# The second block's first norm: weighted x is transposed before its root is known, and the root's factor is applied behind the projections

## The chip, the cores and the metric

The kernel runs as one program on one core of a Trainium2 chip. The metric is the device time of one execution in microseconds (us); of several executions the median is taken. The engines are called as the profile calls them: PE is TensorE's matrix multiply, PEld its weight load, DVE is VectorE, ACT is ScalarE, POOL is GpSimd, SP is SyncE (here it issues the weight loads). Times inside the trace are us from the start of the span.

## The reference

A sequence of 256 tokens of width 1024, everything in float32. The first block has two layers (attention, layer norm, a mixture of 16384 experts called PEER, layer norm). The second block follows on its output:

```python
def rms_norm(x, gain):
    y = xf * lax.rsqrt(jnp.mean(xf * xf, axis=-1, keepdims=True) + NORM_EPS)
    return y * gain

# first_block, last step of its second layer
x = _layer_norm(DEEPNORM_ALPHA * x + ffn, ln_g[layer, 1], ln_b[layer, 1])

# second_block
u = rms_norm(h, attn_pre_norm[l])
mix = hybrid_mixer(u, w_in[l], ...)      # proj = u @ w_in, split into q, k, v, x_lru, g_lru, 2 gates
h = h + rms_norm(mix, attn_post_norm[l])
u = rms_norm(h, mlp_pre_norm[l])
h = h + rms_norm(jnp.square(jax.nn.relu(u @ w_mlp_up[l])) @ w_mlp_down[l], mlp_post_norm[l])
```

The place of the change is the seam between the two blocks: a layer norm, the weighted root mean square norm of its result, and the first projection of `u @ w_in`.

## The kernel before

Tokens lie in two blocks `b` of 128 on the partitions. Each weight of 128x1024 is loaded in float32 (`raw`, four buffers, SP's queue), split into a rounded part `hi` on ACT (L66) and the rest `lo` on DVE (L67), and multiplied in three passes: `hi` with `xh`, `lo` with `xh`, `hi` with `xl`. `xh` and `xl` are the same two parts of the activations, transposed, so that the 1024 features lie on the partitions. The weights come in one fixed list (`plan`); `Stream.next` hands out the next one and splits ahead of it up to two more. The parts have three buffers (`PARTS`), so the `hi` of weight n+3 can only be written when PE is through with weight n. All engines work in the order in which the code is written (a manual schedule); background generators (`bg`) get one step at each `tick`.

A junction between two stages goes like this (`layer_norm`): the last DEFER weights of the projection before are held back for the second block, so that block 0's accumulators end early (`finish`). While PE works on the held matmuls (L182), DVE does block 0's norm. Then come block 0's two halves `h` of 512 columns: four transposes each (L300) into PSUM, a cast to `xh` on ACT (L163) and a subtraction to `xl` on DVE (L164). `half_pass(0)` multiplies block 0 with the first four weights of the next stage (24 matmuls of 512 columns, L157 to L159), while DVE does block 1's norm; `half_pass(1)` does the same for block 1, and in it the next three weights are split.

At three of the junctions of this form the layer norm's own result is transposed. At the one in front of the second block, `begin` returns a function that calls `pre_norm` for each block first: mean square (ACT squares with a sum, L927), root (`rsqrt`: ACT logarithm and exponential, L266 and L267, and one Newton step on DVE, L270 to L273), the product with the gain (L940, L942), the product with the root `pnr` (L944 on DVE for the first half, L945 on ACT for the second), and only then the transposes. `jd` takes the first 512 columns of q (L257); five `proj_half` calls of four weights each do the rest of q, k and v (20 weights, 12 matmuls of 512 columns each, evacuated by ACT at L229 as two tiles); `rope` rotates q and k on DVE (12 small operations, L1033 to L1035) after its half is evacuated. The other four projections (x_lru, the two gates, g_lru) are transposed ones (`proj_t`) and read the same `xh`, `xl`.

`block2` begins with small loads on POOL's queue (cos, sin, the columns `cv`, the mask; L1010 to L1018). The first of them waits for the last matmul of `half_pass(1)`, whose buffers it takes over. Near the end of the mixer POOL's queue loads x (`spill`) and two gains (L1216, L288) for the next norm.

## Time and profile before

| | us |
|---|---|
| median of three runs | 2264.73 (2263.79 to 2266.92) |
| the profiled execution's own time | 2268.64 |
| its span in the trace | 2266.5 |
| PE busy | 2218.0 (98%) |
| DVE busy | 1757.2 (78%) |
| ACT busy | 1229.8 (54%) |

PE is busy nearly all the time, so a stage's time is its matmuls' time unless a wait of PE shows. The three runs spread over 3.1 us. The profiled execution is 3.9 us above their median and its span 1.8 us above; 2.1 us of its time lie outside the span.

### The profile page before, as it was taken

To read this page: it belongs to the slowest core of one execution; us is meant where nothing else is said; L and a number is where in the kernel's file an instruction comes from. 1 tells how busy PE (TensorE), PEld (TensorE's weight loads), DVE (VectorE), ACT (ScalarE), POOL (GpSimd) and SP (SyncE) were. 2 spreads that over 40 slices of the span, in tenths; PEclk is the share of its full clock that TensorE was granted. 3 is DMA by queue.
4 is the path that set the end of the run, shared out by engine and by line. 5 is a ranking of instruction groups with operands and counts; after the bars stand their busy time and mean duration, and the time that the engine had idled before them with its cause. 6 is when DMAs were issued, how large, how long until landed. Compare 5 with 4: busy or idle time off the path is not lost.

```text
span 2266.5 us, 39922 instructions
## 1 busy us (share of the span) xinstructions
PE 2218.0 (98%) x15028; PEld 2000.1 (88%) x15028; DVE 1757.2 (78%) x3501; ACT 1229.8 (54%) x2115; POOL 54.8 (2%) x118
## 2 busy tenths in 40 slices
PE   8999999999999999999999999999999999999998
PEld 7779999999888887888999999888888779997986
DVE  6879998887766668677999988776666857886754
ACT  5744455666445544674445566644555546765643
POOL 4200000000000000000000000000000000000000
PEclk9999999999999999999999999999999999999999
DMA  7556676556777777545667655777777655565664
GB/s 252 156 173 233 218 234 223 201 196 237 253 242 240 243 239 249 185 139 177 226 231 233 216 204 191 255 242 243 243 241 248 218 186 161 178 184 176 214 187 138
DMA packets 151666, 481.96 MB, mean 213 GB/s; under 512 B 17856, under 2 KB 18400, under 8 KB 150192
## 3 DMA queue, kind: packets, MB, share of 16 engines
q1 hardware_dynamic: 126288, 423.09, 57.9%
q10 hardware_dynamic: 19008, 34.61, 4.1%
q0 software_dynamic: 6176, 21.70, 2.7%
q8 instruction: 118, 1.93, 0.3%
q14 instruction: 76, 0.62, 0.1%
HBM read 437.39 MB, written 39.85 MB: 211 GB/s over the span
## 4 chain that ended last, share of the span: by engine, by line
PE 85%; DVE 5%; issue 4%; ACT 3%; DMA 3%; POOL 0%; ACTq 0%; DVEq 0%; SPq 0%; POOLq 0%
PE ps_acc L182 31%; PE ps_h L157 15%; PE ps_h L159 15%; PE ps_h L158 15%; DVE lo L67 1%; PE ps_acc L821 1%; PE ps_acc L822 1%; PE ps_acc L157 1%; PE ps_acc L158 1%; PE ps_acc L159 1%; ACT hi L66 1%; DMA raw<-peer_v 1%; PE ps_acc L705 0%; DMA raw<-peer_w_q 0%; DVE lns L319 0%
## 5 line engine op out<-in xcount | busy, mean ns | idle before, releaser
L67 DVE TENSOR_TENSOR lo<-raw,hi 128x1024 fp32r<-128x1024 f32 x740 | 901.5, 1221 | 415.7 <-ACT hi L66 412.2
L66 ACT CAST hi<-raw 128x1024 fp32r<-128x1024 f32 x740 | 774.6, 1050 | 432.7 <-issue 290.7
L157 PE MATMUL ps_h<-xh,hi 128*128 128x256 f32 x2784 | 788.6, 283 | 1.0 <-ACT k L628 1.0
L159 PE MATMUL ps_h<-xh,lo 128*128 128x256 f32 x2784 | 773.2, 278 | 3.4 <-DVE lo L67 3.3
L158 PE MATMUL ps_h<-xl,hi 128*128 128x256 f32 x2784 | 773.2, 278 | 0.0
L157 PEld LDWEIGHTS ps_h<-xh,hi 128*128 128x128 f32 x2784 | 525.7, 189 | 6.1 <-issue 1.7
L159 PEld LDWEIGHTS ps_h<-xh,lo 128*128 128x128 f32 x2784 | 522.9, 188 | 4.2 <-DVE lo L67 4.2
L158 PEld LDWEIGHTS ps_h<-xl,hi 128*128 128x128 f32 x2784 | 523.3, 188 | 0.2
L182 PE MATMUL ps_acc<-hi,wh 128*128 128x512 f32 x1024 | 318.2, 390 | 3.4 <-ACT wh L163 3.3
L182 PE MATMUL ps_acc<-hi,wo 128*128 128x512 f32 x1024 | 318.0, 390 | 0.1
L182 PE MATMUL ps_acc<-lo,wh 128*128 128x512 f32 x1024 | 317.4, 389 | 0.2 <-DVE lo L67 0.2
L848 ACT ACTIVATE hs<-ps_h 128x256 f32<-128x256 f32 x256 | 98.3, 384 | 343.6 <-PE ps_h L159 176.8
L182 PEld LDWEIGHTS ps_acc<-hi,wh 128*128 128x128 f32 x1024 | 191.5, 188 | 45.6 <-ACT wh L163 6.2
L182 PEld LDWEIGHTS ps_acc<-hi,wo 128*128 128x128 f32 x1024 | 191.7, 188 | 41.4 <-DVE wo L164 1.9
L182 PEld LDWEIGHTS ps_acc<-lo,wh 128*128 128x128 f32 x1024 | 192.1, 188 | 40.6 <-DVE lo L67 0.7
L164 DVE TENSOR_TENSOR wo<-jd,wh 128x256 fp32r<-128x256 f32 x256 | 107.1, 419 | 2.0 <-ACT wh L163 2.0
L872 DVE TENSOR_TENSOR jd<-G,jd 128x256 f32<-128x256 f32 x256 | 106.9, 417 | 2.2 <-ACT G L824 2.2
L163 ACT CAST wh<-jd 128x256 fp32r<-128x256 f32 x256 | 101.7, 397 | 11.0 <-DVE jd L872 10.9
L824 ACT ACTIVATE G<-ps_acc 128x64 f32<-128x64 f32 (+1 forms) x256 | 82.1, 385 | 6.6 <-PE ps_acc L822 1.0
L157 PE MATMUL ps_h<-hi,xh 128*128 128x512 f32 x160 | 68.8, 430 | 9.5 <-ACT hi L66 7.8
L821 PE MATMUL ps_acc<-oh 128*128 128x128 f16 x512 | 69.6, 221 | 0.0
L822 PE MATMUL ps_acc<-oh 128*128 128x128 f16 x512 | 68.6, 219 | 0.0
(358 smaller groups left out, 2372.6 us busy)
## 6 DMA issues: line engine op xcount, KB each, us to landing
raw<-peer_u SPq DMA_DIRECT2D x256, 512.0 KB, 4.5
raw<-peer_v SPq DMA_DIRECT2D x256, 512.0 KB, 4.3
H<-hs SPq DMA_DIRECT2D x128, 256.0 KB, 2.1
jd<-H ACTq DMA_DIRECT2D x128, 256.0 KB, 4.2
raw<-w_in SPq DMA_DIRECT2D x32, 512.0 KB, 3.7
raw<-w_up SPq DMA_DIRECT2D x32, 512.0 KB, 4.0
raw<-w_down SPq DMA_DIRECT2D x32, 512.0 KB, 4.2
raw<-w_qkv SPq DMA_DIRECT2D x24, 512.0 KB, 4.4
```

What stands on the lines that cost most here:

```text
L66: self.nc.scalar.copy(hi, raw)
L67: self.nc.vector.tensor_sub(lo, raw, hi)
L157: mm(out, lh, rh, start=start, stop=False)
L158: mm(out, lh, rl, start=False, stop=False)
L159: mm(out, ll, rh, start=False, stop=stop)
L163: self.nc.scalar.copy(hi, src)
L164: self.nc.vector.tensor_sub(lo, src, hi)
L182: mm(acc[half], x, w[:, half * 512 : half * 512 + 512], start=a, stop=b)
L821: mm(out, o[:, 0, j], o[:, 1, j], start=True, stop=False)
L822: mm(out, o[:, 0, j], o[:, 2, j], start=False, stop=True)
L848: nc.scalar.activation(hs[i // 2][:, i % 2], o, AF.Gelu)
L872: nc.vector.tensor_tensor(w, g[:, i - first], hl[i // 2][:, i % 2], ALU.mult)
```

## The change

`pre_norm` is gone. `norm` takes a function `then` that it calls after each half: it multiplies the layer norm's result with the gain into the buffer `y`, and `y` is transposed without its root. `layer_norm` computes the root's factor aside with `late_factor` (the sums of squares on ACT behind the casts of the same block, the rest of both blocks behind block 1's transposes) into a lasting tile `factor`, and `half_pass` and `proj_half` multiply with it, token by token, when ACT evacuates q, k and v. The transposed projections have the tokens on the free dimension, where a factor for each partition doesn't help; for them `rescale`, a background generator, adds `xh` and `xl`, multiplies with the factor spread over all partitions (`rb`), and splits the product again into `x2`. The factor comes into `rb` by way of DRAM: two small transfers on POOL's queue behind the mask. `x2` lies where x and the two gains are loaded later, so that load now waits for the last matmul that reads `x2`.

```diff
@@ proj_half, half_pass
-            self.nc.scalar.copy(dst[:, b], acc[b])
+            if by is None:
+                self.nc.scalar.copy(dst[:, b], acc[b])
+            else:
+                self.nc.scalar.mul(dst[:, b], acc[b], by[:, b : b + 1])
@@ norm
             nc.vector.scalar_tensor_tensor(x[:, b, s], y[:, s], r, beta[:, s], ALU.mult, ALU.add)
+            if then:
+                then(y, s)
@@ layer_norm
+            def scaled(b):
+                def then(y, s):
+                    u[b] = y
+                    nc.vector.tensor_tensor(y[:, s], x[:, b, s], gain[:, s], ALU.mult)
+
+                return then
+
+            factors = [self.late_factor(pool, x[:, b], self.factor[:, b : b + 1]) for b in range(NB)]
-        u0 = after(0) if after else x[:, 0]
-        n1 = self.norm(pool, 1, acc[1], x, g, beta)
+        n1 = self.norm(pool, 1, acc[1], x, g, beta, scaled(1))
         for h in range(2):
             next(n1)
-            self.transposed(0, h, u0)
+            self.transposed(0, h, u[0])
         self.st.split(self.st.used + NJ, self.st.used)
+        if factors:
+            next(factors[0])
         next(n1)
         self.half_pass(0, tiles)
-        u1 = after(1) if after else x[:, 1]
         for h in range(2):
-            self.transposed(1, h, u1)
-        self.half_pass(1, tiles)
+            self.transposed(1, h, u[1])
+        if factors:
+            next(factors[1])
+            for f in factors:
+                for _ in f:
+                    pass
+        self.half_pass(1, tiles, self.factor if factors else None)
@@ pre_norm (removed)
-        root = self.mean_square(pool, r, [x[:, s] for s in halves], 1e-6)
-        next(root)
-        nc.vector.tensor_tensor(u[:, halves[0]], x[:, halves[0]], gain[:, halves[0]], ALU.mult)
-        next(root)
-        nc.vector.tensor_tensor(u[:, halves[1]], x[:, halves[1]], gain[:, halves[1]], ALU.mult)
-        next(root)
-        nc.vector.tensor_scalar(u[:, halves[0]], u[:, halves[0]], r, None, ALU.mult)
-        nc.scalar.mul(u[:, halves[1]], u[:, halves[1]], r)
@@ block2
+            rx = outer.enter_context(tc.tile_pool(name="b2x", bufs=1, side="right"))
+            x2 = [rx.tile([P, KD, T], F32R, tag=t, name="x2" + t) for t in ("x", "gains")]
+            rd = self.dram.tile([NB, P], F32, tag="rd", name="rd")
+            rb = two.tile([P, 2, T], F32, tag="th", name="rb")[:, 0]
+            nc.gpsimd.dma_start(rd.rearrange("b p -> p b"), self.factor)
+            nc.gpsimd.dma_start(rb, rd.rearrange("b p -> (b p)").unsqueeze(0).to_broadcast([P, T]))
+
+            def rescale():
+                for _ in range(4):
+                    yield
+                for k in range(0, KD, 2):
+                    s = slice(k, k + 2)
+                    z = two.tile([P, 2, T], F32, tag="m2", name=f"xz{k}")
+                    nc.vector.tensor_tensor(z, self.xh[:, s].bitcast(F32), self.xl[:, s].bitcast(F32), ALU.add)
+                    yield
+                    nc.vector.tensor_tensor(z, z, rb.unsqueeze(1).to_broadcast([P, 2, T]), ALU.mult)
+                    self.part(x2[0][:, s], x2[1][:, s], z)
+                    yield
...
-                        self.proj_half(self.xh, self.xl, dst[:, :, half * 512 : half * 512 + 512], "acc")
+                        self.proj_half(self.xh, self.xl, dst[:, :, half * 512 : half * 512 + 512], "acc", self.factor)
...
-                    o = self.proj_t(self.xh, self.xl)
+                    o = self.proj_t(*x2)
...
-            xp = outer.enter_context(tc.tile_pool(name="b2x", bufs=1, side="right"))
-            x = xp.tile([P, NB, D], F32, tag="x", name="x2")
+            x = rx.tile([P, NB, D], F32, tag="x", name="x2")
             nc.gpsimd.dma_start(x, spill)
```

Three places show how the order of instructions moves. The first is DVE at block 0's norm, from the layer norm's first half on (`lny` is the norm's buffer y, `xr` its result, `pnu` the weighted and scaled copy, `mss` the sum of squares, `pnr` the root, `ps_acc` the accumulators, `xl` the small part of the transposed activations). Before:

```order
L329 SCALAR_TENSOR_TENSOR xr_19675<-lny_21194,lnr_21197,gains_20812 128x512
L323 SCALAR_TENSOR_TENSOR lny_21194<-lny_21194,lnm_21196,gains_20812 128x512
L329 SCALAR_TENSOR_TENSOR xr_19675<-lny_21194,lnr_21197,gains_20812 128x512
L940 TENSOR_TENSOR pnu_21217<-xr_19675,gains_20813 128x512
L929 TENSOR_TENSOR mss_21219<-mss_21219 128x1
L268 TENSOR_SCALAR rsx_21224<-mss_21219 128x1
L942 TENSOR_TENSOR pnu_21217<-xr_19675,gains_20813 128x512
L270 SCALAR_TENSOR_TENSOR rsz_21226<-rsy_21225,rsx_21224 128x1
L271 TENSOR_SCALAR rsz_21226<-rsz_21226 128x1
L273 TENSOR_TENSOR pnr_21216<-rsy_21225,rsz_21226 128x1
L944 TENSOR_SCALAR pnu_21217<-pnu_21217,pnr_21216 128x512
L316 SCALAR_TENSOR_TENSOR lny_21236<-xr_19675,ps_acc_18169 128x512
```

Now, at the same place:

```order
L336 SCALAR_TENSOR_TENSOR xr_19676<-lny_21195,lnr_21198,gains_20813 128x512
L351 TENSOR_TENSOR lny_21195<-xr_19676,gains_20814 128x512
L330 SCALAR_TENSOR_TENSOR lny_21195<-lny_21195,lnm_21197,gains_20813 128x512
L336 SCALAR_TENSOR_TENSOR xr_19676<-lny_21195,lnr_21198,gains_20813 128x512
L351 TENSOR_TENSOR lny_21195<-xr_19676,gains_20814 128x512
L323 SCALAR_TENSOR_TENSOR lny_21219<-xr_19676,ps_acc_18170 128x512
L165 TENSOR_TENSOR xl<-ps_m_21224,xh 128x4x128
```

The first half's product with the gain stands right behind the first half of the norm, and nothing of the root stands ahead of block 1's first step (L316 before, L323 now).

The second place is ACT behind block 1's transposes, from the casts to `xh` to the evacuation of `half_pass` (`hi` are weights of the first `proj_half`, `msj` the squares, `fac` the factor). Before:

```order
L163 CAST xh<-ps_m_21323 128x4x128
L163 CAST xh<-ps_m_21330 128x4x128
L66 CAST hi_21344<-raw_21279 128x1024
L66 CAST hi_21354<-raw_21287 128x1024
L66 CAST hi_21364<-raw_21295 128x1024
L257 COPY jd<-ps_h_21272 128x512
L257 COPY jd<-ps_h_21337 128x512
```

Now:

```order
L164 CAST xh<-ps_m_21292 128x4x128
L164 CAST xh<-ps_m_21299 128x4x128
L954 ACTIVATE msj_21306,mss_21307<-xr_19676 128x512 x2
L273 ACTIVATE rsy_21312<-mss_21240,eps1e-06_76 128x1
L274 ACTIVATE rsy_21312<-rsy_21312 128x1
L273 ACTIVATE rsy_21322<-mss_21307,eps1e-06_76 128x1
L274 ACTIVATE rsy_21322<-rsy_21322 128x1
L66 CAST hi_21337<-raw_21268 128x1024
L66 CAST hi_21347<-raw_21276 128x1024
L66 CAST hi_21357<-raw_21284 128x1024
L264 ACTIVATE jd<-ps_h_21261,fac 128x512
L264 ACTIVATE jd<-ps_h_21330,fac 128x512
```

Block 1's squares and both blocks' roots stand ahead of the three weight splits, and the evacuation is a product instead of a copy.

The third place is DVE in the projections of k, from the weights split in the second `proj_half` to its `rope` (`xz` is `rescale`'s buffer z, `x2x` and `x2gains` the two parts of `x2`, `kn` is k). Only rows of the change are new here; before, the four rows `lo` and the `rope` stood alone.

```order
L1048 TENSOR_TENSOR xz_21557<-xh,xl 128x512
L67 TENSOR_TENSOR lo_21562<-raw_21539,hi_21561 128x1024
L1050 TENSOR_TENSOR xz_21557<-xz_21557,rb 128x512
L165 TENSOR_TENSOR x2gains<-xz_21557,x2x 128x512
L67 TENSOR_TENSOR lo_21583<-raw_21559,hi_21582 128x1024
L1048 TENSOR_TENSOR xz_21598<-xh,xl 128x512
L67 TENSOR_TENSOR lo_21603<-raw_21580,hi_21602 128x1024
L1050 TENSOR_TENSOR xz_21598<-xz_21598,rb 128x512
L165 TENSOR_TENSOR x2gains<-xz_21598,x2x 128x512
L1067 TENSOR_TENSOR rm_21623<-kn_21388,cos_21402 128x64
```

Between the weights' small parts there are now an addition, a product that waits for `rb`, and a subtraction that waits for a cast on ACT; the second and the fourth of these sets stand right ahead of a `rope`.

## Rows read from the trace of the kernel before

**Rows 1.** The page: its first line, the busy time of each engine, and the shares of the span in the chain of work that ended last.

```profile
span 2266.5 us, 39922 instructions
PE 2218.0 (98%) x15028; PEld 2000.1 (88%) x15028; DVE 1757.2 (78%) x3501; ACT 1229.8 (54%) x2115; POOL 54.8 (2%) x118
...
PE 85%; DVE 5%; issue 4%; ACT 3%; DMA 3%; POOL 0%; ACTq 0%; DVEq 0%; SPq 0%; POOLq 0%
```

**Rows 2.** The waits of PE between 1780 and 2000 us: who waited for whom, us in total, times, the longest.

```profile
PE ps_m L300 <- DVE pnu L944: 5.1, 2, 3.0
PE ps_h L159 <- DVE lo L67: 3.3, 2, 2.8
```

**Rows 3.** PE's instructions at the seam in order of time: start, duration, engine, line, operation, in brackets the idle time before and what ended it. The held matmuls' last, block 0's transposes, the first matmul of `half_pass(0)`, block 1's transposes, the first matmul of `half_pass(1)`, and the first two of the first `proj_half`.

```profile
1799.33 0.39 PE L182 MATMUL ps_acc<-hi,wo 128*128 128x512 f32 x1
1802.69 1.97 PE L300 MATMUL ps_m<-ident,pnu 128*128 128x128 f32 x8 [2.97 <-DVE pnu L944]
1804.48 0.79 PE L157 MATMUL ps_h<-hi,xh 128*128 128x512 f32 x1
...
1814.35 1.07 PE L300 MATMUL ps_m<-ident,pnu 128*128 128x128 f32 x8 [2.12 <-DVE pnu L944]
1815.66 0.80 PE L157 MATMUL ps_h<-hi,xh 128*128 128x512 f32 x1 [0.24 <-ACT xh L163]
...
1822.82 0.39 PE L157 MATMUL ps_acc<-hi,xh 128*128 128x512 f32 x1
1823.05 0.40 PE L158 MATMUL ps_acc<-lo,xh 128*128 128x512 f32 x1
```

**Rows 4.** Two stretches of 2 us, one in each half pass: the stretch, its length, busy time (and instructions) of PE, PEld, DVE, ACT and POOL, then the granted clock of PE as a share of full speed, the DMA share and GB/s.

```profile
1804.00:1806.00 2.00, 2.00 (x8) 1.45 (x7) 1.54 (x3) 1.01 (x2) 0.00 (x0) 0.50 0.00 0
...
1816.00:1818.00 2.00, 2.00 (x6) 1.48 (x6) 1.86 (x3) 2.00 (x4) 0.00 (x0) 0.50 0.00 0
```

**Rows 5.** DVE's instructions at the seam in order of time, with the columns of rows 3.

```profile
1797.60 0.75 DVE L329 SCALAR_TENSOR_TENSOR xr<-lny,lnr,gains 128x512 f32<-128x512 f32 x1
1798.27 0.74 DVE L323 SCALAR_TENSOR_TENSOR lny<-lny,lnm,gains 128x512 f32<-128x512 f32 x1
1799.05 0.75 DVE L329 SCALAR_TENSOR_TENSOR xr<-lny,lnr,gains 128x512 f32<-128x512 f32 x1
1799.72 0.68 DVE L940 TENSOR_TENSOR pnu<-xr,gains 128x512 f32<-128x512 f32 x1
...
1805.66 0.68 DVE L164 TENSOR_TENSOR xl<-ps_m,xh 128x512 fp32r<-128x512 f32 x1
1806.26 1.27 DVE L319 BATCH_NORM_STATS2 lns<-lny 128x6 f32<-128x512 f32 x2
...
1809.17 0.75 DVE L329 SCALAR_TENSOR_TENSOR xr<-lny,lnr,gains 128x512 f32<-128x512 f32 x1
...
1817.07 3.50 DVE L67 TENSOR_TENSOR lo<-raw,hi 128x1024 fp32r<-128x1024 f32 x3
```

**Rows 6.** PE's instructions at two junctions of the same form without the weighted norm: the first layer's (from 129 us) and the second layer's (from 1029 us). Columns as in rows 3.

```profile
129.06 0.66 PE L300 MATMUL ps_m<-ident,x 128*128 128x128 f32 x4 [1.36 <-DVE x L329]
...
131.23 0.40 PE L158 MATMUL ps_h<-lo,xh 128*128 128x512 f32 x1
...
1029.27 0.63 PE L300 MATMUL ps_m<-ident,x 128*128 128x128 f32 x4 [0.87 <-DVE x L329]
1029.66 0.48 PE L157 MATMUL ps_h<-hi,xh 128*128 128x512 f32 x1
...
1035.62 0.60 PE L300 MATMUL ps_m<-ident,x 128*128 128x128 f32 x4
```

**Rows 7.** ACT's instructions at the seam: squares with a sum, the root's logarithm, the product with the root, the three weight splits, and a copy out of PSUM. Columns as in rows 3.

```profile
1809.96 0.63 ACT L927 ACTIVATE msj<-xr 128x512 f32<-128x512 f32 x1 [1.61 <-DVE xr L329]
...
1812.42 0.29 ACT L266 ACTIVATE rsy<-mss,eps1e-06_76 128x1 f32<-128x1 f32 x1 [0.23 <-DVE mss L929]
...
1813.72 0.72 ACT L945 ACTIVATE pnu<-pnu,pnr 128x512 f32<-128x512 f32 x1 [0.77 <-DVE pnr L273]
...
1815.98 2.95 ACT L66 CAST hi<-raw 128x1024 fp32r<-128x1024 f32 x3
...
1823.02 0.59 ACT L257 COPY jd<-ps_h 128x512 f32<-128x512 f32 x1 [3.60 <-PE ps_h L159]
```

**Rows 8.** The second `proj_half` ends (tiles of k): ACT's evacuation of two tiles, then DVE's row `lo` before the `rope`, the first of the `rope`'s twelve operations, and the next `lo`. Columns as in rows 3.

```profile
1844.31 1.27 ACT L229 COPY kn<-ps_acc 128x512 f32<-128x512 f32 x2 [1.01 <-PE ps_acc L159]
...
1843.33 1.23 DVE L67 TENSOR_TENSOR lo<-raw,hi 128x1024 fp32r<-128x1024 f32 x1 [1.52 <-ACT hi L66]
1844.93 0.22 DVE L1033 TENSOR_TENSOR rm<-kn,cos 128x64 f32<-128x64 f32 x1 [0.37 <-ACT kn L229]
...
1846.87 1.22 DVE L67 TENSOR_TENSOR lo<-raw,hi 128x1024 fp32r<-128x1024 f32 x1
```

**Rows 9.** POOL's queue: the first of the small loads and the mask behind them, and the later load of x. Columns as in rows 3.

```profile
1823.53 0.54 POOL L1010 DMA_DIRECT2D cos<-c_cos  x1 [11.32 <-DMA raw<-w_qkv]
...
1827.81 0.59 POOL L1018 DMA_DIRECT2D mask<-c_mask  x1
...
1946.78 0.53 POOL L1216 DMA_DIRECT2D x<-xs  x1 [0.36 <-issue]
```

**Rows 10.** DMA issues of the whole run: what is written from what, the queue, how many, KB each, median us from issue to landing.

```profile
tri_in<-c_tri POOLq DMA_DIRECT2D x1, 128.0 KB, 5.7
...
gcol<-subln SPq DMA_DIRECT2D x1, 0.5 KB, 3.6
```

More of the change, by code (lines that the diff above doesn't have):

```diff
@@ L238, in junction, with half_pass @@
         return ctx
-    def half_pass(self, b, tiles):
+    def half_pass(self, b, tiles, by=None):
         acc = self.ps("h")
@@ L256, in half_pass @@
             for i, ps in enumerate(self.passed):
-                self.nc.scalar.copy(self.jd[:, i, :512], ps)
+                if by is None:
+                    self.nc.scalar.copy(self.jd[:, i, :512], ps)
+                else:
+                    self.nc.scalar.mul(self.jd[:, i, :512], ps, by[:, i : i + 1])
             self.passed = []
@@ L304, in transposed, with norm @@
         self.part(xh[sl], xl[sl], v)
-    def norm(self, pool, b, acc, x, g, beta):
+    def norm(self, pool, b, acc, x, g, beta, then=None):
         nc = self.nc
@@ L329, in norm, with layer_norm @@
             nc.vector.scalar_tensor_tensor(x[:, b, s], y[:, s], r, beta[:, s], ALU.mult, ALU.add)
+            if then:
+                then(y, s)
         yield
[L332 to L339 removed]
+    def layer_norm(self, pool, acc, x, g, beta, gain=None):
+        nc, tiles, factors = self.nc, [], []
+        if gain is not None:
+            u = [None] * NB
+            def scaled(b):
[4 more added lines that the diff above has]
+            factors = [self.late_factor(pool, x[:, b], self.factor[:, b : b + 1]) for b in range(NB)]
+        else:
+            u, scaled = [x[:, b] for b in range(NB)], lambda b: None
+        for _ in self.norm(pool, 0, acc[0], x, g, beta, scaled(0)):
+            pass
+        n1 = self.norm(pool, 1, acc[1], x, g, beta, scaled(1))
         for h in range(2):
             next(n1)
[L342 removed]
+            self.transposed(0, h, u[0])
         self.st.split(self.st.used + NJ, self.st.used)
+        if factors:
+            next(factors[0])
         next(n1)
         self.half_pass(0, tiles)
[L346 removed]
         for h in range(2):
[L348 to L349 removed]
+            self.transposed(1, h, u[1])
[5 more added lines that the diff above has]
+        self.half_pass(1, tiles, self.factor if factors else None)
     def plan(self):
```

28 lines of the change are left out of this document (12 added, 16 removed).

## The prediction

> **What bounds the kernel now.** I began with the page: PE is busy for 98% of the span and has 85% of the chain that ended last [rows 1]. So a change pays what it takes out of PE's waits, or out of matmuls that run at a low clock, and nothing else. Next came PE's waits around the seam: the largest are two on the weighted, scaled copy `pnu`, 5.1 us together; a wait for a weight's small part, 2.8 us at most, lies elsewhere [rows 2]. In order of time PE ends the held matmuls at 1799.72, stands for 2.97 us, transposes block 0, multiplies, stands for 2.12 us, transposes block 1, and starts `half_pass(1)` at 1815.66 and the first `proj_half` at 1822.82 [rows 3]. [...] DVE is what PE waits for: from 1797.60 on it works through norm, product, root and scaling almost without a gap [rows 5].
>
> **The change, part by part.** All starting times are put beside those of before.
>
> *Block 0.* From DVE's rows I take three spacings: 0.78 us to an operation that needs the one right ahead of it (1798.27 to 1799.05), 0.67 us behind a norm step that isn't needed next (1797.60 to 1798.27), 0.60 us behind a two-tensor operation (1805.66 to 1806.26) [rows 5]. The new order gives: norm half 1797.60, product with the gain 1798.38 (ready 1799.06), centre 1798.98, norm half 1799.76, product 1800.54 (ready 1801.22). The first half's transposes follow the held matmuls without a wait, the second's start at about 1801.4, and `half_pass(0)` 0.39 us later (1029.27 to 1029.66 [rows 6]), at 1801.8 instead of 1804.48. Block 1's first step on DVE comes at 1801.14; with it, its second half and two subtractions (four operations, 0.60 us apart) the statistics start at 1803.54 instead of 1806.26: 2.7 us won.
>
> *Block 1.* From the statistics to the first norm half it was 1809.17 - 1806.26 = 2.91 us [rows 5], so that half comes at 1806.45, its product at 1807.23, and after 0.60, 0.78 and 0.78 us the second product at 1809.39, ready at 1810.07. [...] The last four transposes start at about 1810.2, `half_pass(1)` at 1810.6 instead of 1815.66: **5.06 us won**. Here the root, 1.3 us from its logarithm to the scaling (1812.42 to 1813.72 [rows 7]), the scaling itself and the squares have left the path.
>
> *The clock.* PE now stands for about 1.2 us ahead of block 0's second half and 1.55 us ahead of block 1's. Before, 2.97 and 2.12 us were followed by half clock; elsewhere a wait of 1.36 us and the one after it were followed by matmuls of 0.40 us, full clock, and one of 0.87 us too [rows 3, 4, 6]. 1.55 us is nearer to 1.36 than to 2.12, so I take full clock: `half_pass(1)` lasts 5.96 us and ends at 1816.6 instead of 1822.82, 6.2 us won by then.
>
> *What the root costs where it went.* On ACT the squares of block 1 (two of about 0.7 us with the reading of their sums), then two roots, stand ahead of the three weight splits that the first `proj_half` needs. The last cast to `xh` ends at 1811.45, the squares at 1812.9, the first root at 1814.15, the second's exponential at 1814.85. The first `hi` is done 1.05 us later, at 1815.9, its `lo` 1.22 us after that, at 1817.15. PE's second matmul of that weight needs it: 1817.2 instead of 1823.05. So 0.4 us of the clock's gain goes back, and **5.85 us** stay. The next two `lo` come 1.14 us apart [rows 5], against 2.75 us in which PE uses up a weight (12 matmuls, 0.23 us apart, 1822.82 to 1823.05 [rows 3]); they are not late.
>
> *Evacuations.* Ten copies of 128x512 out of PSUM and two of `half_pass` become products. A copy takes 0.59 us, a product with a factor 0.72 us from SBUF [rows 7]; no row has one from PSUM, so 0 to 0.13 us more each. I take the middle; PE has four accumulators there for two in use, so it is hidden, but it delays the `rope` behind it. [...]
>
> *Rescale.* Four times: an addition (0.60 us of DVE), and a set of product, cast on ACT and subtraction, 0.68 + 0.58 + 0.60 and hand-overs, 1.95 us in DVE's order. DVE has 2.75 - 1.14 = 1.6 us per weight to spare and two weights of lead, so a single set is hidden. The tight place is sets two to four, which come with two `rope`s (1.94 us: 1844.93 to 1846.87 [rows 8]). In before's times: the cast of set two waits for both evacuations (from 1844.31 [rows 8]), so the next `lo`, at 1846.87 before, starts at 1848.7. From there to the `lo` of the fifteenth weight DVE has four `lo` (4.6 us), two additions (1.2), a set with a wait for the `hi` behind its cast (2.35), a full set (1.95) and a `rope` (1.94): 12.0 us, so it ends at 1848.7 + 12.0 + 1.2 = 1861.9. PE wants it at 1822.82 + 14 x 2.747 + 0.23 = 1861.5. I charge **0.5 us**; bounds 0 (hand-overs shorter, evacuations as fast as the copy) and 2.
>
> *The factor's way to `rb`.* The mask was issued at 1827.81, 4.3 us behind the queue's first load, which waits for the end of `half_pass(1)` [rows 9]. That end moves by 6.2 us, so the two new transfers follow at 1822.1. Nearest rows: 0.5 KB in pieces of 4 bytes takes 3.6 us, 128 KB into all partitions 5.7 us [rows 10]. With 3.6 to 5.7 us each and 0.5 us of issue, `rb` is there between 1829.8 and 1834. DVE's first product that reads it comes at about 1833.2, and the `lo` behind it has 2.5 us to spare: free.
>
> *x and the gains* were loaded at 1946.78 [rows 9]; now they wait for the last projection of g_lru, some 55 us later, and are needed 65 us after that. I take nothing.
>
> *Sum.* 5.06 + 1.2 (clock) - 0.4 (first `lo`) - 0.5 (fifteenth `lo`) = 5.4 us. The stages behind keep their spacing, so the end moves by as much: the span from 2266.5 to 2261.1. The profiled execution was 3.9 us above the median of the runs, so I put the difference against the median: 2264.73 - 5.4 = **2259.3**.
>
> **The rivals.** A measurement of this kernel can tell about 0.2%, 4.5 us, from no change.
>
> 1. *As above*: 2259.3, with the bounds of the small terms 2258.3 to 2260.4. Chance 0.60.
> 2. *The clock falls all the same.* If `half_pass(1)` still takes 7.16 us it ends at 1817.8, later than the first `lo`, and only the 5.06 us count: 2264.73 - 5.06 + 0.5 = 2260.2. For it: two waits lie close together, and 1.55 us is longer than any in rows 6. Against it: those rows. 0.15.
> 3. *DVE runs full in the projections.* Were each of the four sets late by 0.5 to 1 us on PE's clock instead of one, the loss is 2 to 4 us: about 2262. For it: DVE has no gap there in my count from 1846 to 1861. Against: two weights of lead. 0.11.
> 4. *Given back later.* The later load of x and gains (2 MB) meets the weights of the next stage, or a stage that DVE bounds has slack that swallows the start: about 2264.7. Before, the same 2 MB met the projections and no wait of PE for a weight came of it there [rows 2]. 0.10.
> 5. *Slower: `rb` is late.* Its product stands in DVE's order ahead of every `lo`, so PE stops for as long as it is late beyond 1835.7. The gain of 5.9 us is gone at 1841.6; it is slower by 0.2% from 1846.1, which needs 24 us for the two transfers, against 7.7 to 12. Price there: 2269.3. 0.04.
>
> **How the numbers follow.** The predicted time is the first case's. Both first cases lie near the bound of 2260.2: of the first I count 0.85 as faster by over 0.2%, of the second half: 0.51 + 0.08 = 0.59; with a little for a better fall of the small terms 0.60. Slower by over 0.2%: 0.04. The rest, 0.36, is within it. The range takes in cases 1 to 3 and the spread of medians, about 1 us: 2257.6 to 2263.0, and leaves out cases 4 and 5. The likeliest case's own range is 2258.3 to 2260.4.
>
> **What would show it.** Right: block 0's first transposes with no wait, waits of PE of 1.2 and 1.55 us instead of 2.97 and 2.12 (in place of the waits on L944, waits on the product with the gain), granted clock 1.00 in both half passes, `half_pass(1)` 5 us earlier, a wait of PE for `lo` of about half a microsecond at the first and at the fifteenth weight. Wrong: clock 0.50 again; waits of PE for `lo` at most weights of k; DVE waiting for `rb`; the seam 6 us shorter and a later stage longer by as much.

## The result, and the profile after

The changed kernel takes 2298.56 us (median of 4 runs, 2296.18 to 2300.15) where the kernel before takes 2265.01 (4 runs): a ratio of 1.0147, 95% interval 1.0134 to 1.0159. It is about 33 us **slower**. The prediction was 2259.3 us with a range up to 2263.0 and 4 in 100 for slower. The two profiled executions differ by less, 29.5 us of span, because the one before was 3.6 us above its runs' median and the one after 0.8 below. Every ratio below is against runs of the kernel before on the chip of that experiment, whose medians lie between 2264.07 and 2267.08 us.

The page of the profiled execution after: the busy times of the engines, and the three groups of the narrow matmuls (busy us, mean ns of one).

```profile
span 2296.0 us, 39935 instructions
...
PE 2245.3 (98%) x15028; PEld 2025.1 (88%) x15028; DVE 1766.0 (77%) x3511; ACT 1232.2 (54%) x2117; POOL 57.0 (2%) x120
...
L158 PE MATMUL ps_h<-xh,hi 128*128 128x256 f32 x2528 | 723.0, 286 | 0.9 <-ACT k L655 0.9
L160 PE MATMUL ps_h<-xh,lo 128*128 128x256 f32 x2528 | 709.8, 281 | 0.1
L159 PE MATMUL ps_h<-xl,hi 128*128 128x256 f32 x2528 | 709.4, 281 | 0.0
```

PE is busy for 27 us more than in [rows 1], with the same number of matmuls, and 98% of the span as before. So most of what was lost is no waiting: the same work takes longer.

PE at the seam after, columns as in [rows 3]:

```profile
1823.89 0.60 PE L307 MATMUL ps_m<-ident,lny 128*128 128x128 f32 x4
1825.61 0.66 PE L307 MATMUL ps_m<-ident,lny 128*128 128x128 f32 x4 [1.12 <-DVE lny L351]
...
1832.41 0.63 PE L307 MATMUL ps_m<-ident,lny 128*128 128x128 f32 x4 [0.20 <-DVE lny L351]
1834.58 0.63 PE L307 MATMUL ps_m<-ident,lny 128*128 128x128 f32 x4 [1.55 <-DVE lny L351]
1834.97 0.48 PE L158 MATMUL ps_h<-hi,xh 128*128 128x512 f32 x1
...
1840.67 0.40 PE L158 MATMUL ps_acc<-hi,xh 128*128 128x512 f32 x1
```

The end of the held matmuls, 1799.72 before, is 1823.9 here: **24.3 us were lost before the seam was reached**, in a part of the program in which the diff changes no instruction. Counted from the start of the last held matmul (1799.33 before, 1823.66 after), `half_pass(1)` starts at 11.31 us where it started at 16.33, and the first `proj_half` at 17.01 where it started at 23.49. The first input projection then starts at 82.96 where it started at 78.43. So the seam gave 6.5 us, and what lies between it and the input projections took 11.0.

PE's waits from 1795 to 1915 us after, DVE's from 1836 to 1872, PE's instructions behind the longest wait, and the granted clock in `half_pass(1)` and at that wait (stretch, length, busy time and instructions of PE, PEld, DVE, ACT and POOL, clock, DMA share, GB/s):

```profile
PE ps_acc L158 <- ACT hi L66: 6.5, 1, 6.5
PE ps_m L307 <- DVE lny L351: 2.9, 3, 1.5
PE ps_acc L159 <- DVE lo L67: 0.5, 1, 0.5
```

```profile
DVE xz L1050 <- DMA rb<-rd: 10.2, 1, 10.2
```

```profile
1870.04 0.79 PE L158 MATMUL ps_acc<-hi,xh 128*128 128x512 f32 x1 [6.46 <-ACT hi L66]
1871.30 0.79 PE L159 MATMUL ps_acc<-lo,xh 128*128 128x512 f32 x1 [0.47 <-DVE lo L67]
...
1875.16 0.40 PE L159 MATMUL ps_acc<-lo,xh 128*128 128x512 f32 x1
```

```profile
1836.00:1838.00 2.00, 2.00 (x10) 1.63 (x9) 1.08 (x5) 1.57 (x6) 0.00 (x0) 1.00 0.81 328
...
1863.00:1883.00 20.00, 13.07 (x47) 9.81 (x46) 12.66 (x25) 8.82 (x11) 0.00 (x0) 0.83 0.48 156
```

DVE waits 10.2 us for `rb`, ACT's cast of the rescaled x behind it, `hi` casts behind that, and PE stands for 6.5 us. The clock is 0.83 of full on average over the 20 us that begin with this wait; between the levels 1.00 and 0.50 that is 34% of 20 us, 6.8 us, at half clock. It falls while PE still stands (0.79 from 1867 to 1869, 0.50 from 1869 to 1873), so only a part of that costs time: the ten matmuls from 1870.04 to 1875.16 take 5.12 us for 2.33 us at the 0.233 us of their neighbours, 2.8 us more, 0.5 of it a second wait for a `lo`.

So two things had to be explained: 24 us in the first block, and 10 us behind the seam.

### The profile page after: what moved, and what is told of

It reads as the page before. It is cut to its first block, busy times and chain, and to the rows that moved or that the text cites. A ratio compares the mean times of both kernels' runs of the same rounds, so it can differ in the third digit from the quotient of the medians.

```text
span 2296.0 us, 39935 instructions
## 1 busy us (share of the span) xinstructions
PE 2245.3 (98%) x15028; PEld 2025.1 (88%) x15028; DVE 1766.0 (77%) x3511; ACT 1232.2 (54%) x2117; POOL 57.0 (2%) x120
## 4 chain that ended last, share of the span: by engine, by line
PE 84%; DVE 5%; issue 4%; DMA 4%; ACT 3%; POOL 0%; ACTq 0%; DVEq 0%; SPq 0%; POOLq 0%
PE ps_acc L183 31%; PE ps_h L158 15%; PE ps_h L160 15%; PE ps_h L159 15%; DVE lo L67 1%; PE ps_acc L848 1%; PE ps_acc L849 1%; ACT hi L66 1%; PE ps_acc L159 1%; PE ps_acc L160 1%; PE ps_acc L158 1%; PE ps_acc L732 0%; DMA rd<-fac 0%; DVE rr L1143 0%; DMA zsq<-zq 0%
## 5 line engine op out<-in xcount | busy, mean ns | idle before, releaser
L158 PE MATMUL ps_h<-xh,hi 128*128 128x256 f32 x2528 | 723.0, 286 | 0.9 <-ACT k L655 0.9
L160 PE MATMUL ps_h<-xh,lo 128*128 128x256 f32 x2528 | 709.8, 281 | 0.1
L159 PE MATMUL ps_h<-xl,hi 128*128 128x256 f32 x2528 | 709.4, 281 | 0.0
L158 PEld LDWEIGHTS ps_h<-xh,hi 128*128 128x128 f32 x2528 | 477.0, 189 | 5.9 <-issue 1.7
L159 PEld LDWEIGHTS ps_h<-xl,hi 128*128 128x128 f32 x2528 | 477.0, 189 | 0.1
L160 PEld LDWEIGHTS ps_h<-xh,lo 128*128 128x128 f32 x2528 | 476.4, 188 | 0.5 <-DVE lo L67 0.5
L164 ACT CAST wh<-jd 128x256 fp32r<-128x256 f32 x256 | 102.0, 398 | 10.2 <-DVE jd L899 10.2
L158 PE MATMUL ps_h<-hi,xh 128*128 128x512 f32 x160 | 67.0, 419 | 8.8 <-ACT hi L66 7.9
L160 PE MATMUL ps_h<-x2x,lo 128*128 128x256 f32 x256 | 72.6, 284 | 2.5 <-DVE lo L67 2.5
L158 PE MATMUL ps_h<-x2x,hi 128*128 128x256 f32 x256 | 73.9, 289 | 0.0
```

The source lines that it names most:

```text
L158: mm(out, lh, rh, start=start, stop=False)
L159: mm(out, lh, rl, start=False, stop=False)
L160: mm(out, ll, rh, start=False, stop=stop)
L164: self.nc.scalar.copy(hi, src)
```

## The first loss: where a tile lies

The pace of the narrow matmuls is the distance of their starts. The same place in the first up stage (`proj_t`, L157 to L159 before, L158 to L160 after), before and after; nine spacings lie between the first and the last row shown of each:

```profile
183.74 0.28 PE L159 MATMUL ps_h<-xh,lo 128*128 128x256 f32 x1
...
184.76 0.28 PE L159 MATMUL ps_h<-xh,lo 128*128 128x256 f32 x1
```

```profile
185.82 0.28 PE L160 MATMUL ps_h<-xh,lo 128*128 128x256 f32 x1
...
186.88 0.28 PE L160 MATMUL ps_h<-xh,lo 128*128 128x256 f32 x1
```

1.02 / 9 = 113 ns before, 1.06 / 9 = 118 ns after. Averaged over the narrow matmuls of the two up stages, which take the weights `peer_u` (L157 to L159 on `xh`, `xl`; spacings without a wait) it is 114.72 before and 118.5 after. Summed over the roughly 6,600 of them ahead of the seam, with those of the other projections, 25.9 us. No instruction there is new. What the diff does change is the allocation: `self.factor` is a new tile of 8 bytes (32 with its padding) between `eps` and `ident`, and by the allocator's addresses in the built programs all tiles behind it move by 32 bytes, among them both parts of every weight (hi, lo). The tiles ahead of it, `xh`, `xl` and `jd`, stay.

Theory 1 was therefore: the shift costs the 24 us, and the late `rb` what is lost behind the seam. The rivals: something else in the change slows the first block; or a single tile other than the weights' parts.

**e1 and e2: undo the shift, make the shift alone.**

```
e1 (after):  self.factor = c.tile([P, 16], F32, ...)[:, :NB]     # 64 bytes
e2 (before): self.pad = c.tile([P, 2], F32, ...); gpsimd.memset  # ahead of ident
```

> The changed kernel, with one difference: the tile of the two root factors takes 64 bytes of each SBUF partition where it took 8 (padded to 32), so that every tile allocated behind it starts at a multiple of 64 bytes again where it did in the kernel before. Theory 1 (the 32-byte shift of the weight tiles makes each matmul with stationary weights slower, and the rest of the loss lies behind the seam, where the row of factors comes late): the 24 us that the changed kernel had lost before the seam, and the 3 us in the input projections of the second block, come back, so 2298.6 - 24.3 - 3.0 = about 2271 us (2267 to 2273). Theory 2 (the slowdown of the first block comes from something else in the change, not from where its tiles lie): no difference, 2298 us. Theory 3 (only the place counts, and nothing is lost behind the seam): 2259 to 2261 us, as predicted.

> The kernel before, with one unused tile of 8 bytes (padded to 32) allocated where the changed kernel allocates the factors. Nothing reads it, and one GpSimd memset writes it at the start. Theory 1 (place of the weight tiles): slower by the 24.3 us lost before the seam and the 3.0 us of the input projections, 2265.0 + 27 = about 2292 us (2288 to 2294), and the matmuls of the first block's key and value stages stand 0.119 us apart in place of 0.113. Theory 2 (something else in the change): 2265 us.

e2: 2295.74 us, ratio 1.0148 (1.0132 to 1.0164). One unused tile slows the first block as the change did: its two up stages take 407.7 and 405.9 us, in the kernel after 406.9 and 407.3, before 395.7. So the shift is enough, and nothing else of the change is needed for the first loss. That the two totals agree as well is partly chance, since e2 has neither the gain at the seam nor the loss behind it; e2 lies 1.7 us above the range I gave. e1: 2303.63 us, 1.0182 (1.0167 to 1.0198), and the up stage's pace is about 119.2 ns. So my form of the theory fell: a multiple of 64 bytes doesn't bring the pace back, it is worse than 32.

**e3: only the parts.**

```
pool "pad0" (32 bytes) | pool "parts" (hi, lo) | pool "pad1" (32 bytes)
```

> The kernel before, with two unused 32-byte tiles, one ahead of the pool that holds the weights' two parts (hi, lo) and one behind it: the parts lie at 32 modulo 64, everything ahead of them where it lay, and everything behind them 64 bytes further, at the same place modulo 64. Theory 1a (TensorE reads a stationary 128x128 tile from hi or lo more slowly when it starts at 32 modulo 64): the whole loss shows, about 2292 us (2287 to 2294). Theory 1b (another tile's place is what counts: the raw weights, the identity, or the tiles of the stages behind the parts): 2265 us, and a value between tells a shared loss.

2315.79 us, 1.0233 (1.0217 to 1.0249): more than the whole shift. The up stages go from 395.7 to 406.5 us, as in e2 (407.7 and 405.9). But the down stages (weights `peer_v`), which no run had touched, take 362.7 and 354.7 us for 353.6 and 344.7. There the parts are the moving operand and `wh`, `wo` the stationary one. In e2 both had moved by 32 bytes; in e3 the parts moved by 32 and `wh`, `wo` by 64. The group of the wide matmuls in e3, and in the kernel after (mean ns of one behind the busy us):

```profile
L186 PE MATMUL ps_acc<-hi,wh 128*128 128x512 f32 x1024 | 324.4, 396 | 3.4 <-ACT wh L167 3.3
```

```profile
L183 PE MATMUL ps_acc<-hi,wh 128*128 128x512 f32 x1024 | 318.1, 390 | 3.5 <-ACT wh L164 3.3
```

That pointed to the distance between the two operands of a matmul, not to the place of one.

**p1: a probe.** The up stage's sequence of matmuls alone, with operands at chosen places.

> A probe in place of the whole computation: nothing of the reference is computed. It runs the up stage's matmul sequence alone (per k: hi times xh, hi times xl, lo times xh; stationary 128x128, moving 128x256; 72 matmuls a stretch, 3 stretches a setting, two transposes between stretches), without transfers beside it. In the settings w0 to w480 the stationary parts start 0, 32, ... 480 bytes behind a multiple of 512 and the moving x at a multiple of 512; in x32 to x128 the moving x is shifted in place of the parts; in b32 and b64 both by the same; v0 to v224 have stationary x and moving 128x512 parts, with the parts shifted. In the kernel before the parts lie 64 bytes behind x modulo 128 and the trace has two paces, 113.5 and 117.8 ns a matmul; with 96 (e2, e3) 117.3 and 118.7; with 128 (e1) 118.7 alone. Theory 1 (what counts is where the stationary tile starts against the moving one, within TensorE's own two reads): w64 gives 113.5 or 117.8 ns, w96 117.3 or 118.7, w128 118.7, with nothing else running; x shifts act as w shifts of the opposite sign, and b32 and b64 as w0. Theory 2 (TensorE is slowed by other engines' or transfers' accesses, whose banks change with the shift): one pace in all settings. Theory 3 (the absolute start of the stationary tile counts): b32 as w32, and the x settings as w0.

The third and the last matmul of a stretch of 72, in some of the settings (69 spacings between the two rows of each). First `hi`, `lo` 0, 64, 128 and 224 bytes behind a multiple of 512, then x shifted by 64 instead, then both shifted by 64:

```profile
20.84 0.28 PE L159 MATMUL w0x<-xh,lo 128*128 128x256 f32 x1
...
29.11 0.28 PE L159 MATMUL w0x<-xh,lo 128*128 128x256 f32 x1
...
73.46 0.28 PE L159 MATMUL w64x<-xh,lo 128*128 128x256 f32 x1
...
81.59 0.28 PE L159 MATMUL w64x<-xh,lo 128*128 128x256 f32 x1
...
125.85 0.28 PE L159 MATMUL w128x<-xh,lo 128*128 128x256 f32 x1
...
134.04 0.28 PE L159 MATMUL w128x<-xh,lo 128*128 128x256 f32 x1
...
204.70 0.28 PE L159 MATMUL w224x<-xh,lo 128*128 128x256 f32 x1
...
212.74 0.28 PE L159 MATMUL w224x<-xh,lo 128*128 128x256 f32 x1
...
466.59 0.28 PE L159 MATMUL x64x<-xh,lo 128*128 128x256 f32 x1
...
474.72 0.28 PE L159 MATMUL x64x<-xh,lo 128*128 128x256 f32 x1
...
572.26 0.28 PE L159 MATMUL b64x<-xh,lo 128*128 128x256 f32 x1
...
580.53 0.28 PE L159 MATMUL b64x<-xh,lo 128*128 128x256 f32 x1
```

That is 119.9, 117.8, 118.7, 116.5, 117.8 and 119.9 ns. All settings, by distance (start of the stationary tile less start of the moving one, modulo 256), from all starts in the trace:

| distance, bytes | 0 | 32 | 64 | 96 | 128 | 160 | 192 | 224 |
|---|---|---|---|---|---|---|---|---|
| parts shifted by 0 to 224 | 120.0 | 118.2 | 117.8 | 118.7, 117.4 | 118.7 | 119.9 | 117.8 | 116.6 |
| parts shifted by 256 to 480 | 120.0 | 118.2 | 117.8 | 118.7, 117.4 | 118.7 | 119.9 | 117.8 | 116.6 |
| x shifted by 32 to 128 | | | | | 118.7 | 120.0 | 117.8 | 116.7, 117.8 |
| both shifted by 32, 64 | 119.9 | | | | | | | |

With no transfer at work (DMA share 0.00 from 70 to 78 and from 87 to 95 us), and no other engine but ScalarE (a copy of about 0.4 us in 8 us), the pace goes with the distance of the operands modulo 256 bytes, from 116.6 to 120.0 ns; at one and the same distance the paces lie 1.3 ns apart at most (118.7 and 117.4 at 96). Why the distance counts isn't shown. Theories 2 and 3 of the probe fall, its theory 1 stands, but for one thing: 113.5 ns doesn't show. Without it distance 64 would be no better than 192 and worse than 224, so what the kernel before had over its shifted copies hangs on that faster pace (p2 below). In the wide form (stationary x, moving 128x512) distance 0 is best: 226.8 ns, against 229.2 where the parts stand 64 bytes behind x and 232.4 to 234.1 elsewhere. That is e3's down stage. In the kernel before the parts stand 64 bytes behind x; in e2 and after 96; in e1 128.

**g2: the same 32 bytes, ahead of x.**

```
self.pad = c.tile([P, 2], F32, ...)   # ahead of self.xh
```

> The kernel before with e2's unused 32-byte tile, allocated ahead of x (xh, xl) and not behind it: x, the weights' parts and all behind them move by 32 bytes together, so that every distance between a moving and a stationary operand stays as it was. If the distance modulo 256 is what counts, as the probe's b32 and b64 say: as the kernel before, 2264 to 2268 us, with 113.5 and 117.8 ns in the first block's key and value stages, where e2, with the same tile behind x, was 1.5% slower. If the absolute place counts: as e2, about 2295 us.

2264.96 us, 1.0001 (0.9991 to 1.0012). The tile that costs 1.5% behind `xl` costs nothing ahead of `xh`.

**h1: a distance that no kernel had.** e2's tile with 160 bytes, so that the parts lie 224 behind x.

> The kernel before with e2's unused tile at the same place, 160 bytes long and not 32: the weights' parts lie 224 bytes behind x modulo 256, a distance that no kernel so far had in the first block. The probe gives 116.7 ns at 224, one pace. In the kernel before the 8149 matmuls of this form that the trace shows without a wait stand 114.83 ns apart on average, so the table says 8149 x (116.7 - 114.83) = 15 us more, 2264.5 + 15 = about 2280 us (2277 to 2283), about half of what e2's 32 bytes cost. If the probe's levels don't carry over to the kernel and any shift costs as much as e2's or e1's: 2295 to 2304 us. If only shifts that aren't a multiple of 64 cost (which e1 speaks against): 2295.

2285.23 us, 1.0083 (1.0066 to 1.0100). Above the range I gave, but between the kernel before and e2. The order of the four distances (64, 224, 96, 128) is the table's if distance 64 counts with the kernel's 114.83 and not with the probe's 117.8. The pace in the kernel was 117.04 ns, not the probe's 116.7; 8149 x (117.04 - 114.83) = 18 us against 19 measured.

**p2: the two paces at distance 64.** The average 114.72 of the kernel before is made of stretches at 113.5 and at 117.8 ns, which change only where transposes stand between matmuls.

> A second probe, nothing of the reference is computed: the up stage's matmul sequence at distance 64, groups of 24 in two PSUM banks in turn as in the kernel, in stretches of 6 and 7 groups, with 1, 2, 3 or 4 transposes between stretches, and then with a pause in which TensorE waits for VectorE. In the kernel before, the pace at this distance is 117.8 or 113.5 ns, and changes at pairs of transposes alone. If the pace that a stretch has is set by what stands ahead of it, both paces show, and which one follows the number of transposes or the number of groups. If the 113.5 ns need something of the kernel that is not here (other engines or transfers), 117.8 shows throughout.

Windows of 10 us inside two neighbouring stretches with four transposes between them (length, PE's busy time and instructions, clock, DMA share, GB/s):

```profile
453.00:463.00 10.00, 10.00 (x87) 1.00 0.00 0
471.00:481.00 10.00, 10.00 (x90) 1.00 0.01 2
```

Each count has two or three matmuls that began before the window; from the starts, 117.8 and 113.4 ns. Both paces show with hardly a transfer (DMA share 0.00 and 0.01) and no other engine but ScalarE at work (1.45 and 1.49 of the 10 us), at full clock (1.00), and in this probe a stretch keeps its pace until the next interruption. With one, two, three and four transposes, 5 of 8, 2 of 8, 4 of 8 and 7 of 8 stretches had the fast one, with a pause 5 of 6. What chooses is **not settled**: neither the number of transposes nor the length of the stretch does.

## The second loss: the row of factors

**e5: write the factors first.**

```
rd <- factor | cos, sin, cv, mask | rb <- rd | gb        # order on GpSimd's queue
```

> The changed kernel with the factors' tile of 64 bytes, as in e1, and the order of GpSimd's transfers at the seam changed: the factors are written to DRAM ahead of cos, sin, cv and the mask, and read back as a row (rb) ahead of the two operations that wait for cv. Theory 1 (rb's lateness stops VectorE, then ScalarE's hi casts, then TensorE for 6.5 us and half a clock behind it): rd issues at about 1840 where it issued at 1849.8, rb lands about 9 us earlier (in the changed kernel's times 1858 in place of 1867.7), TensorE doesn't wait for hi there, and the time is the one predicted, 2258 to 2261 us, 5 us under the kernel before and 6 to 9 us under e1. Rival (VectorE and ScalarE have no room for the rescaling in the q, k, v projections, whenever rb comes): as e1, at most 2 us under it.

2307.59 us, 1.0197 (1.0183 to 1.0211): 4 us more than e1, where I expected 6 to 9 less. PE now stands for `lo`, and DVE ahead of it for `cos`:

```profile
PE ps_acc L159 <- DVE lo L67: 7.0, 1, 7.0
...
```

```profile
DVE rm L1067 <- DMA cos<-c_cos: 10.2, 1, 10.2
```

The transfers of that stretch in e5 (KB each, us to landing), then those of the kernel after, and its queue of weights in 8 us ahead of and in 8 us beside the way of `rd` (packets, MB, share of 16 engines):

```profile
mask<-c_mask POOLq DMA_DIRECT2D x1, 192.0 KB, 13.1
...
rd<-fac POOLq DMA_DIRECT2D x1, 1.0 KB, 9.3
cos<-c_cos POOLq DMA_DIRECT2D x1, 16.0 KB, 12.1
```

```profile
mask<-c_mask POOLq DMA_DIRECT2D x1, 192.0 KB, 4.2
rb<-rd POOLq DMA_DIRECT2D x1, 128.0 KB, 7.3
...
cos<-c_cos POOLq DMA_DIRECT2D x1, 16.0 KB, 3.9
...
rd<-fac POOLq DMA_DIRECT2D x1, 1.0 KB, 10.3
```

```profile
q1 hardware_dynamic: 436, 1.59, 55.7%
```

```profile
q1 hardware_dynamic: 125, 0.45, 84.5%
```

And f1 below, which has no `rd`, from 1826 to 1834 us:

```profile
q1 hardware_dynamic: 441, 1.61, 63.1%
```

From 1843 to 1851 us a packet of the weights holds an engine for 0.557 x 8 x 16 / 436 = 0.16 us, from 1854 to 1862, with `rd` on its way (issued 1849.81, landed by 1860.1), for 0.845 x 8 x 16 / 125 = 0.87 us; in f1 it is 0.631 x 8 x 16 / 441 = 0.18 us. So `rd` doesn't just land late; what moves beside it is slow too: `cos` takes 12.1 us behind it and 3.9 us ahead of it. That is why putting it first lost. My expectation for f3 below speaks of 256 packets of 4 bytes. The factors are 256 numbers of 4 bytes, but the trace has `rd` as 16 packets of 64 bytes, and why 1 KB takes 10 us and slows its neighbours is not settled.

**f0, f1, f3: all tiles at their old places.** The factors lie in the padding of an `eps` tile. f0 changes nothing else. f1 makes the row without DRAM. f3 keeps f0's transfers and starts the rescaling later.

```
f0: t = c.tile([P, 1 + NB], ...); eps, self.factor = t[:, 0:1], t[:, 1:]
f1: fb[:, b] = factor[:, b] spread | ps <- transpose(fb[:, b]) | rb <- ps    # no rd, no transfer
f3: for _ in range(10): yield          # 4 in f0
```

> The changed kernel with the two factors kept in a part of the second eps tile that was padding, so that every other tile lies where it lay in the kernel before. Theory 1: the first block's pace comes back whole, w_qkv's first load stands at 1780.6 as before, and what is left is the seam (5 us gained) and the late row of factors (up to 8 us lost, less where its wait falls better): 2262 to 2268 us. Theory 2 (something else in the change slows the first block): 2298 us.

> As f0 (all tiles at their old places), and the row of factors is made without DRAM: VectorE spreads each factor over 128 columns, TensorE transposes the two tiles, ScalarE copies them out of PSUM, at three steps of the background in the q, k, v projections; the two transfers are gone. Theory 1 (the late row is the second loss, and without it the prediction's sum holds): 2258 to 2261 us, no wait of TensorE above 1 us between the second half pass and the first input projection. Rival (the rescaling itself overfills VectorE or ScalarE there): 2263 us or more, with waits for hi or lo.

> f0 (the changed kernel with every tile at its old place, the factor row through DRAM as in the changed kernel), but the rescaling of x starts six background steps later, so that VectorE and ScalarE reach the first product with the row when it has landed. If only the queueing of VectorE and ScalarE behind the row costs time: the 4.7 us wait for hi is gone and the time is as f1's, 4 to 6 us under f0, ratio to the kernel before 0.998 to 1.000. If the transfers themselves cost time as well (256 packets of 4 bytes hold up the weights and cos behind them), less than that comes back. If the rescaling needs the place of those six steps, VectorE gets full at the end of the projections, and the time is f0's or more.

f0: 2270.73 us, 1.0010 (0.9990 to 1.0029). The first block's stages are back to the kernel before's within 2 us (the up stages 396.3 and 396.1 us for 395.7), so the 24 us were the place alone. f1: 2265.95 us, 0.9994 (0.9985 to 1.0003). f3: 2265.20 us, 0.9998 (0.9989 to 1.0007). f0 and f1 lie above the ranges I gave, and by these ratios f3 is 2.7 us under f0, not 4 to 6. So with both losses gone, in f1 and f3, the time is that of the kernel before within the noise, and not 5 us less. PE's waits from 1795 to 1915 us in f0 and in f3, and f0's clock behind its wait (columns as above):

```profile
PE ps_acc L158 <- ACT hi L66: 4.7, 1, 4.7
...
```

```profile
1840.00:1860.00 20.00, 17.32 (x64) 13.71 (x65) 16.64 (x36) 12.38 (x16) 0.00 (x0) 0.83 0.50 148
```

```profile
PE ps_m L307 <- DVE lny L351: 2.9, 3, 1.5
```

From the last held matmul to the first input projection it is 78.43 us before, 80.51 in f0 and 72.34 in f3. The late row cost 8.2 us in f0: 4.9 from start to start at the wait, 3.2 in the eleven matmuls behind it (2.7 of half clock, 0.5 of another wait for a `lo`), and 0.1 at a later one. With the rescaling six steps later both are gone with the same transfers, and VectorE has the room: f3's seam is 6.1 us shorter than before. So the queueing behind the row was the cost. f1 by the other way has 75.48, 3.1 us more than f3: its added transposes and their wait of 1.5 us for VectorE's copies take 1.7, 0.7 are lost ahead of `half_pass(0)`, and 0.5 at the `lo` of the fifteenth weight.

**What is left of f3's 6.1 us.** Its profiled span is 3.4 us shorter than before (2263.1 for 2266.5); by time the gain is 0.5 us, interval -1.6 to 2.5. So in the traces 2.7 us are given back behind the start of the input projections, all of it by 2000 us. About half is again a place: `x2` stands at distance 224 from the parts, and its 733 unhindered matmuls run at 116.9 ns where those on `xh` had 114.1 in that stage, 2.1 us, of which shorter waits return some. The other 1.35 us are clock: in f3 a wait of PE of 2.46 us for a `lo` is followed by half clock from 1982.5 to 1985.9; before, the wait at the same place is 2.78 us long and the clock stays full.

**g1: place the second block's tiles by the table.**

```
(f1 +)  rx.tile([P, 24], ...)                  # x2 to distance 64
        factor = fp.tile([P, 64], ...)[:, :NB]  # later pools from 224 to 192 modulo 256
        yield                                   # between copies and transposes
```

> f1 (factor row made by TensorE, old places) with three edits. A pad of 96 bytes in the pool of the rescaled x puts it 64 bytes ahead of the weights' parts modulo 256 (f1: parts 224 behind, 117 ns); a pad of 224 bytes behind the second root's factor puts the pools of the second block's later stages at 192 modulo 256 where they were at 224: the moving 128x512 weights then have distance 0 to the stationary tiles of the out and down projections (probe: 226.7 ns for 233.0), and the branch projections have 192 (117.8 for 119.9). One step of the background lies between VectorE's copies of the factors and TensorE's transposes. If the probe's table holds in the kernel: down 111.1 to about 109 us (384 matmuls by 5 to 6 ns), the input projections 127.5 to about 126, the 1.5 us wait for the copies gone, together 4 to 5 us under f1, a ratio of 0.997 to the kernel before. If distances do not add up so in the kernel: as f1.

2255.76 us, 0.9960 (0.9947 to 0.9974): faster than both kernels, 8.6 us by the medians. The down projection (moving parts, `uh` stationary) before and in g1:

```profile
L182 PE MATMUL ps_acc<-hi,uh 128*128 128x512 f32 x128 | 41.0, 394 | 0.0
```

```profile
L183 PE MATMUL ps_acc<-hi,uh 128*128 128x512 f32 x128 | 40.4, 390 | 0.0
```

Spacing 232.1 to 226.7 ns (probe: 233 to 227), the stage 111.2 to 109.1 us. The branch projections' matmuls on `ah` go from 119.9 to 117.8, exactly the table's values for 160 and 192, and those on `x2` from 117.0 to 115.1. The profiled execution of g1 is the longest of its five (2266.7 us), so its span isn't compared. By the ratios g1 is 7.7 us under f1, where 4 to 5 were forecast; its faster executions have no trace, so the surplus stays unexplained.

## Why the prediction was wrong, point by point

- **The seam: right.** Forecast: `half_pass(1)` 5.06 us earlier. It is 16.33 - 11.31 = 5.02. The waits were to be about 1.2 and 1.55 us; the largest are 1.12 and 1.55.
- **The clock: right here, with luck.** It stayed full through both half passes, 1.00 on average from 1823 to 1843; the first `proj_half` starts 6.48 us earlier, forecast 6.2. The 5.96 us that the sum takes for `half_pass(1)` are the 24 matmuls from 1029.66 to 1035.62 in [rows 6]; it took 5.70 (1834.97 to 1840.67), and 7.16 before, at 0.50 from 1816 to 1818 [rows 4]. But the length of a wait, from which I argued, didn't decide it. At the first layer's junction [rows 6] waits of 1.36 and 0.79 us left the clock full before; in f0 the same two, 1.35 and 0.79 us, were followed by half clock. In g1 the two waits of this seam, 1.32 and 1.54 us, were too, and `half_pass(1)` took 7.04 us for 5.70. That is rival 2, in one of seven traces with the new seam. Before and f0 at the first layer's junction, then g1 in `half_pass(1)`:

```profile
132.00:134.00 2.00, 2.00 (x10) 1.59 (x9) 2.00 (x4) 0.00 (x0) 0.00 (x0) 1.00 0.00 0
```

```profile
132.00:134.00 2.00, 2.00 (x6) 1.60 (x5) 1.96 (x4) 0.00 (x0) 0.00 (x0) 0.50 0.00 0
```

```profile
1814.00:1816.00 2.00, 2.00 (x6) 1.51 (x6) 0.91 (x3) 1.96 (x6) 0.00 (x0) 0.50 0.98 401
```

- **The first `lo`: right.** 0.4 us forecast, 0.4 lost; the 0.5 us for `lo` in the list of waits is a later one, at 1871.30.
- **The fifteenth `lo`: right where the row is in time.** In f1 and g1 PE loses 0.5 us at that weight, as forecast, and in the kernel after 0.2. f3, with its later rescaling, has no wait there; its seam gains 6.1 us, the sum said 5.4 with this half microsecond in it. Rival 3, all four sets late, is not there: in f1 the fifteenth `lo` is the only late one of those behind a set.
- **The evacuation: within its bounds.** A product out of PSUM takes 0.687 us (median of four of `kn`: 0.684; of `v`: 0.688), the row bounds were 0.59 and 0.72 [rows 7]. A plain copy out of PSUM had 0.586 before (median of four of `kn` and of `v`).
- **`rb` "free": the second step that failed. The mechanism was there, as rival 5, but its transfers were mis-sized.** I took 3.6 to 5.7 us for each from [rows 10] and had the row landed by 1834; `rd` took 10.3 us and `rb` 7.3. `rd` also issued 3.4 us later than I had it (1822.1), mainly because the load of `cv` ahead of it kept POOL waiting for 4.86 us, 2.29 before. In the kernel after `rd` issues at 1849.81, `rb`'s first reader starts at 1867.70, 17.9 us later (in the times of before, less 24.3 us, at 1843.4). Rival 5 had PE stop for as long as the row is late beyond 1835.7, 7.7 us; 6.5 was measured. It took the whole gain to be gone at 1841.6; f0's reader comes at 1841.2 in the times of before, and f0's seam is 2.1 us longer, because I had left out the slow clock behind such a wait (2.7 us in f0). The 3.6 us of the small load in [rows 10] were no measure for a small store beside a stream of weights.
- **"The stages behind keep their spacing": the step that failed most.** The sum starts at the seam: it takes the stages ahead of it as unchanged and those behind it as shifted, and has no term for the allocation, without a reason given. The tile of 8 bytes for `factor`, which the diff as printed above doesn't show, cost about 24 us before the seam (e2, f0). After, `x2` itself also stands at distance 0 (119.9 ns on 747 matmuls, 4.3 us more than `xh`'s 114.1 in that stage).
- **The later load of x and the gains: nothing**, as forecast; no wait of PE names it.

The span's 29.5 us are 24.3 ahead of the seam, 4.5 in it and in the projections behind it, and 0.7 from there to the end. The 4.5 are -6.5 at the seam, 6.6 from start to start at the wait for `hi`, 2.8 behind it, 0.4 and 0.2 at the first and the fifteenth `lo`, and 1.0 for 225 wide matmuls at 233.3 ns for 228.9. The 0.7 hide two things: up to the end of the mixer the kernel after loses 2.7 us, mostly by `x2`'s place, and at the next junction it gains 2.2, because there the kernel before runs at half clock (0.50 from 2076 to 2078) and the kernel after doesn't (1.00 from 2104 to 2112).

## What to carry to other kernels

A tile that is added to a pool moves every tile behind it, so compare the addresses of two programs before comparing their times; where a matmul-bound stage changes pace without a new instruction (here from 114.72 to 118.5 ns), look at the distance of its two operands. A small tile can go ahead of both operands (g2) or into padding that is there already (f0). A column of scalars that was wanted as a row took some 14 to 18 us through memory beside a stream of weights; what waits for it should be issued late enough not to block the queue in front of the bottleneck (f3). And a forecast that counts on the clock should carry both of its levels: like waits (1.36 and 1.35 us) were followed by either.

## What was not expected of the hardware

- In the probe p1 the spacing of 128x128 by 128x256 matmuls went with the distance of their operands' starts modulo 256 bytes, from 116.6 to 120.0 ns. For 128x512 it was 226.8 at 0 and up to 234.1 elsewhere. The differences showed without transfers, at a DMA share of 0.00.
- At distance 64 the probe p2 had two paces, 113.4 and 117.8 ns, at the same full clock (1.00). One of them was kept until PE was interrupted. What chooses it stayed open.
- A store of 1 KB (16 packets of 64 bytes) took 8 to 10 us; while it was on its way a packet of the weights took 0.87 us for 0.16, and a 16 KB load behind it 12.1 us for 3.9.
- Waits of PE of like length were followed by full clock in one execution and half clock in another: 1.36 us (before) and 1.35 (f0) at one junction, 2.78 (before) and 2.46 (f3) at one projection.
